# Half-size weight sums moved to VectorE, squares to ScalarE, and seven products for four more chunks of the MLP

## The chip, the cores and the metric

One core of a Trainium2 chip runs the whole program. The metric is the device time of one launch in microseconds, as the median of several runs.

## The reference

Two layers work on x, 512 rows of 1024 numbers in float32. Each layer computes three kinds of attention from x, merges them by gates, projects the result and normalises. Then comes the MLP, which is what this change touches:

```
ff = square(relu(x @ w_up[layer])) @ w_down[layer]
x = layer_norm(alpha * x + ff, ln2_g[layer], ln2_b[layer])
```

`w_up` is 1024 x 4096 and `w_down` is 4096 x 1024.

## The kernel before, in words

**Numbers.** TensorE multiplies in a rounded float32 format. To keep float32 precision, each operand is held as a rounded part and a remainder (`Split`, line 42), and each product is three matmuls, hi by hi, hi by lo and lo by hi (`mm3`, lines 152 to 155). A full matmul has 128 x 128 stationary numbers and 512 moving columns.

**The stream of weights.** All weights come through one list (`Stream`, line 164). A weight of 128 x 1024 is loaded into a `raw` tile (two exist), split by ScalarE into `whi` (line 182) and by VectorE into `wlo` (line 183), and taken by the matmuls. There are five pairs of `whi` and `wlo` in one pool and three in another, so splits may run up to eight weights ahead. `take` (line 213) hands out one weight, and through `advance` (line 201) it writes down the next split and the next load. An entry of the list may also be a function, which then makes its own tile; `Fast` uses that.

**The MLP of a layer.** The 4096 hidden features go in four quarters of eight chunks of 128 (loop at line 898). For each chunk m, 24 matmuls make `psu` (line 933), and `hidden` (line 901) turns it into stationary operands: ScalarE applies Relu (line 910), VectorE squares in place (line 911), and the result lies in `f`, of which one buffer exists for a pair of chunks. In the first quarter the first four chunks are done in two halves of tokens (`cut`, line 925), so that their results come close together.

**The down projection.** In quarters 0 to 2 it uses seven products of halves in place of eight (`Fast`, line 765): the matrix of hidden values and the weights are each cut in two by two blocks, and seven products of sums of blocks are enough. The sums of the hidden blocks are made on VectorE in `hidden` (lines 918 to 922). The sums of weight blocks are made by GpSimd, one subtraction of two 128 x 1024 tiles at a time, in place (`operand`, line 784, subtraction in line 796):

```
dst, a, b = ((b11, None, None), (b11, b12, b11), (b11, b22, b11), (b22, None, None),
             (b12, b22, b12), (b12, None, None), (b11, b12, b11))[i]
if a is not None:
    nc.gpsimd.tensor_tensor(dst, a, b, op=ALU.subtract)
```

A quarter loads eight `w_fast` tiles and uses 14 weights (seven products, two tiles each). `run` (line 802) makes each product with two times four times three matmuls and adds it from PSUM to x (`add_stats`, line 259, on VectorE), two sums per product. The first product needs, as its fourth stationary operand, the slice that `hidden` makes of chunk 6.

In the last quarter all eight chunks go the plain way (`token_major`, line 737): 8 chunks, 4 token blocks, 2 halves, 3 matmuls each. The first four weights are used one after the other, the last four are held, so that the token blocks end one by one and their normalisation starts early.

**What sets the order.** Per engine the program order, with the list of weights as written in lines 855 to 859; loads are issued from the queue of SyncE (SP). The tile framework places independent instructions of one engine earlier or later when it builds the program.

**Places in memory.** Small tiles are rounded up to 64 bytes (`LINE`, line 39), so every tile starts at a multiple of 64 bytes.

Of the kernel before, what the change touches and what calls it, by code (L numbers as in the profile page):

```python
# [17 lines left out]
P = 128  # L18
L = 2
# [17 lines left out]
C_OFF = {0: 0, 1: 256, 2: 640, 3: 1024}  # L37
C_WID = 1280
LINE = 16


class Split:
# [84 lines left out]

@with_exitstack
def encoder(ctx: ExitStack, tc: tile.TileContext, x, x_t, w_qkv, w_c, w_gate, b_gate, qn, kn, rpb,
            w_ba, w_bb, w_bc, w_out, ln1_g, ln1_b, w_up, w_down, w_fast, ln2_g, ln2_b,  # L130
            mask_a, rope_a, rope_b, out):
    nc = tc.nc
    const = ctx.enter_context(tc.tile_pool(name="const", bufs=1))
# [1 line left out]
    glob = ctx.enter_context(tc.tile_pool(name="glob", bufs=1))  # L135
    dram = ctx.enter_context(tc.tile_pool(name="dram", bufs=1, space=bass.MemoryType.DRAM))
    edge = ctx.enter_context(tc.tile_pool(name="edge", bufs=1, side="right"))
    edge.tile([P, LINE // 2], F32, name="edge")
    psum = ctx.enter_context(tc.tile_pool(name="psum", bufs=8, space=bass.MemoryType.PSUM))

    def bank(name):
# [2 lines left out]
    def f32(ap):  # L144
        return ap.bitcast(F32)

    ident = const.tile([P, P], F32, name="ident")
    make_identity(nc, ident)
    nhalf = const.tile([P, 16], F32, name="nhalf")
    nc.vector.memset(nhalf, -0.5)  # L150

    def mm3(ps, lhs, rhs, start, stop, again=False):
# [145 lines left out]
    def attention(l, keep, qk, open_heads):  # L298
# [72 lines left out]
        def norm_rotate(tb):  # L371

            raw = raws["b"][:, tb]
            r = raw.rearrange("p (h d) -> p h d", d=HD)
            sq = pool.tile([P, 10, HD], F32, tag="sq", name="sq", bufs=2)
            nc.scalar.activation(sq, r, AF.Square)
            cs = pool.tile([P, 2, 2, HD], F32, tag="cs", name="cs", bufs=1)
            nc.vector.tensor_tensor(cs, gqk, ropeb[:, :, tb][:, None].to_broadcast([P, 2, 2, HD]), op=ALU.mult)
            yield 1
            ss = pool.tile([P, 2, LINE], F32, tag="ss", name="ss", bufs=2)[:, :, :10]  # L380
            nc.vector.tensor_reduce(ss[:, 0], sq, axis=AX.X, op=ALU.add)
            nc.vector.tensor_scalar(ss[:, 0], ss[:, 0], 1.0 / HD, RMS_EPS, op0=ALU.mult, op1=ALU.add)
# [127 lines left out]
        def scores(name, h, qb):  # L510
            ks, qs = pairs[name, h // 2]
            q, k = qs[h % 2], ks[h % 2]
            k0, k1 = keys_of(name, qb)
            n = (k1 - k0) * P
            ps = bank("pss")[:, :n]
            nc.tensor.matmul(ps, q[:, qb * P:(qb + 1) * P], k.hi[:, k0 * P:k1 * P], start=True, stop=False)
            nc.tensor.matmul(ps, q[:, qb * P:(qb + 1) * P], k.lo[:, k0 * P:k1 * P], start=False, stop=True)
            p = pool.tile([P, S], F32, tag="p", name="p", bufs=4)[:, :n]
            st = pool.tile([P, LINE], F32, tag="stat", name="stat", bufs=4)
            if name == "b":  # L520
                s = ps
# [12 lines left out]
            return p, normalize  # L534
# [115 lines left out]
        with tc.manual_schedule() if l == 0 else nullcontext():  # L650
            work.flush()
        pool = open_heads()
        hb = keep.tile([P, 4 * KB], F32, tag="hb", name="hb")[:, :3 * KB]
        nc.sync.dma_start(hb, b_gate[l])
        nc.vector.tensor_scalar(hb, hb, 0.5, None, op0=ALU.mult)
        gqk = pool.tile([P, 2, 2, HD], F32, tag="gqk", name="gqk", bufs=1)
# [108 lines left out]
    class Fast:  # L765
# [6 lines left out]
        ORDER = ((1, 0, "x", (0, 0)), (4, 1, "z", (1, 1)), (5, 2, "x", (0, 1)), (7, 3, "z", (0, 1)),  # L772
                 (6, 4, "x", (1, 1)), (3, 5, "y", (0, 0)), (2, 6, "x", (1, 0)))

        def __init__(self, pools, src):
            self.pools, self.src = pools, src
            self.b = {}

        def load(self, quarter, half, into):
            t = self.pools["mlp"].tile([P, 1024], F32, tag=f"b{into}{half}", name="braw")  # L780
            nc.sync.dma_start(t, self.src[quarter, half])
            self.b[into, half] = t

        def operand(self, i, half):

            if i == 0 and half == 0:
                for quarter in (0, 1, 3):
                    for h in range(2):
                        self.load(quarter, h, quarter)
            if i == 5:  # L790
                self.load(2, half, 1)
            b11, b12, b22 = (self.b[k, half] for k in (0, 1, 3))
            dst, a, b = ((b11, None, None), (b11, b12, b11), (b11, b22, b11), (b22, None, None),
                         (b12, b22, b12), (b12, None, None), (b11, b12, b11))[i]
            if a is not None:
                nc.gpsimd.tensor_tensor(dst, a, b, op=ALU.subtract)  # L796
            return dst

        def items(self):
            return [lambda i=i, half=half: self.operand(i, half) for i in range(7) for half in range(2)]  # L800

        def run(self, hid, done):
            ps = {}
            for a, _, name, (i, n) in self.ORDER:
                w = [stream.take(2) for _ in range(2)]
                new = name not in ps
                if new:
                    ps[name] = [bank("psd") for _ in range(2)]
                for t in range(2):
                    for j in range(4):  # L810
                        lhs = hid[j].map(lambda h: h[:, a - 1, t * P:(t + 1) * P])
                        mm3(ps[name][t], lhs, w[j // 2][:, j % 2], new and j == 0, j == 3, True)
# [24 lines left out]
    for l in range(L):  # L837
        with ExitStack() as left:
# [12 lines left out]
            extra[0] = pool(right, "wts", "right")  # L851
            stream.plan([w_out[l, k] for k in range(KB)], [0] * 4 + [1] * 3 + [0])
            pools = {}
            fast = [Fast(pools, w_fast[l, q]) for q in range(3)]
            plan = []
            for q in range(4):
                plan += [w_up[l, q * 8 + m] for m in range(8)]
                plan += fast[q].items() if q < 3 else [w_down[l, m] for m in range(8)]
            stream.plan(plan, [int(m % 8 in (1, 4, 6)) for m in range(len(plan) - 4)] + [1] * 3 + [0])
            if l < L - 1:  # L860
                stream.plan([w_qkv[l + 1, i] for i in range(6)])
# [36 lines left out]
            for q in range(4):  # L898
                hid, sums = [], []

                def hidden(m, ps):
# [6 lines left out]
                    a = 2 * (m % 2)  # L908
                    r = f[:, a:a + 2]
                    nc.scalar.activation(r, ps.rearrange("p (a n) -> p a n", a=2), AF.Relu)  # L910
                    nc.vector.tensor_tensor(r, r, r, op=ALU.mult)
                    if q == 3:
                        split_psum(h.map(lambda t: t[:, a:a + 2]), r)
                    elif a == 0:
                        split_psum(h.map(lambda t: t[:, 0]), f[:, 1])
# [8 lines left out]
                for m0 in range(0, 8, 4):  # L924
                    cut = [(0, 2), (2, 4)] if q == 0 and m0 == 0 else [(0, 4)]
                    ws, ps = [], []
                    for a, b in cut:
                        for i in range(4):
# [8 lines left out]
                            elif i in (0, 2):  # L937
                                late.popleft()()

                if q < 3:  # L940
                    def add(tb, n, ps):
                        add_stats(mlp, xs[tb], ps, n, 1.0 if (tb, n) in started else ALPHA, None)
                        started.add((tb, n))

                    fast[q].run(sums, add)
                    continue

                st = [stats_tile(mlp) for _ in range(TB)]
# [13 lines left out]
                        late.popleft()()  # L962

                stream.burst = 2
                whole = [h.map(lambda t: t[:, 2 * i:2 * i + 2].rearrange("p a n -> p (a n)")) for h in sums for i in range(2)]
                token_major(whole, 8, half_done, done, between)
                stream.burst = 1
    right.close()

# [52 lines left out]
    return w.reshape(k // P // per, per, P, n).transpose(0, 2, 1, 3).reshape(-1, P, 1024)  # L1022


def _quarters(w):

    w = w[:, :24 * P].reshape(L, 3, 2, 2, 2, P, 2, 512).transpose(0, 1, 4, 6, 2, 5, 3, 7)
    return w.reshape(L, 3, 4, 2, P, 1024)


def _swap(g):
# [50 lines left out]
```

## Time and profile before

| | |
|---|---|
| median of 3 runs | 1533.81 us (1532.96 to 1535.28) |
| the profiled execution | 1538.57 us, of which 1536.8 us from the first to the last instruction |
| TensorE (PE) busy | 1501.1 us, 98% |
| VectorE (DVE) busy | 1096.1 us, 71% |
| ScalarE (ACT) busy | 688.0 us, 45% |
| GpSimd (POOL) busy | 311.6 us, 20% |

PE is the matmul engine, PEld its loads of stationary operands. The names `psd<-whi,hh` mean: written tile, then the tiles read. `psu` is the up projection, `psd` an output or down projection, `psg` a gate, `hh` and `hl` the two parts of a hidden operand, `braw` a `w_fast` tile, `raw` any other weight. L183 is line 183. TensorE's own durations overlap, so its pace is read from the starts of the matmuls.

### The profile page before, as it was taken

The page shows a single profiled execution, that of the slowest core. Times are in us where ns is not written, and L with a number is a line of the kernel's source. Part 1 is how long each engine was busy: PE and PEld are TensorE (multiplying, and loading weights), DVE is VectorE, ACT ScalarE, POOL GpSimd, SP SyncE. Part 2 cuts the span into 40 slices and gives each one's busy share as a digit, 9 for nine tenths or more (in the row PEclk, how much of TensorE's full clock was granted, in tenths as well). Part 3 has the DMA queues.
Part 4 walks back from the last instruction along what each step waited for, and adds up shares of the span by engine and source line. Part 5 has one row for each costly group of instructions (what it writes and reads, how often), then busy time and mean ns, then how long its engine had stood idle before and what let it go on. Part 6 is the DMA issues. An engine that isn't in the chain of part 4 may idle for free.

```text
span 1536.8 us, 19258 instructions
## 1 busy us (share of the span) xinstructions
PE 1501.1 (98%) x7256; PEld 1255.7 (82%) x7256; DVE 1096.1 (71%) x1722; ACT 688.0 (45%) x1096; POOL 311.6 (20%) x238
## 2 busy tenths in 40 slices
PE   7999999999998999999999999999999989999997
PEld 6888888888896888888888888888888968888886
DVE  4677977745588797964666787876447888979636
ACT  4565656533134343433236556565332343535320
POOL 0112212311142222210101141233111413222001
PEclk9999999999998999999999999999999999999999
DMA  6222321143242415042331323112441342340411
GB/s 218 84 79 70 112 68 53 58 164 118 75 178 81 139 56 164 1 131 85 114 129 56 99 77 110 55 55 76 160 133 56 152 137 83 91 129 28 138 55 55
DMA packets 43438, 150.63 MB, mean 98 GB/s; under 512 B 5073, under 2 KB 5713, under 8 KB 43345
## 3 DMA queue, kind: packets, MB, share of 16 engines
q1 hardware_dynamic: 43344, 149.40, 30.8%
q8 instruction: 57, 0.93, 0.2%
q14 instruction: 37, 0.30, 0.1%
HBM read 145.19 MB, written 4.19 MB: 97 GB/s over the span
## 4 chain that ended last, share of the span: by engine, by line
PE 88%; DVE 7%; ACT 2%; issue 1%; DMA 1%; POOL 0%; SPq 0%; POOLq 0%; DVEq 0%; ACTq 0%
PE psd L153 8%; PE psd L154 8%; PE psd L155 8%; PE psu L154 6%; PE psu L153 6%; PE psu L155 6%; PE psg L155 6%; PE psg L154 6%; PE psg L153 6%; PE psp L547 3%; PE psq L153 2%; PE psq L155 2%; PE psq L154 2%; DVE wlo L183 2%; PE psb L155 2%; PE psb L153 2%
## 5 line engine op out<-in xcount | busy, mean ns | idle before, releaser
L183 DVE TENSOR_TENSOR wlo<-raw,whi 128x1024 fp32r<-128x1024 f32 (+1 forms) x198 | 247.9, 1253 | 204.2 <-ACT whi L182 201.9
L182 ACT ACTIVATE whi<-raw 128x1024 fp32r<-128x1024 f32 (+1 forms) x198 | 207.7, 1051 | 268.7 <-DMA raw<-in_w_up 110.6
L153 PE MATMUL psu<-xTh,whi 128*128 128x512 f32 (+1 forms) x576 | 210.8, 366 | 0.0
L154 PE MATMUL psu<-xTl,whi 128*128 128x512 f32 (+1 forms) x576 | 210.7, 366 | 0.0
L155 PE MATMUL psu<-xTh,wlo 128*128 128x512 f32 (+1 forms) x576 | 210.4, 365 | 0.0
L153 PE MATMUL psd<-whi,hh 128*128 128x512 f32 x464 | 183.2, 395 | 14.8 <-ACT hh L231 14.8
L796 POOL TENSOR_TENSOR braw<-braw 128x1024 f32<-128x1024 f32 x48 | 130.1, 2713 | 332.7 <-DVE wlo L183 169.2
L154 PE MATMUL psd<-wlo,hh 128*128 128x512 f32 x464 | 182.3, 393 | 0.0
L155 PE MATMUL psd<-whi,hl 128*128 128x512 f32 x464 | 182.2, 393 | 0.0
L153 PE MATMUL psg<-xTh,whi 128*128 128x512 f32 x384 | 156.7, 408 | 0.0
L155 PE MATMUL psg<-xTh,wlo 128*128 128x512 f32 x384 | 151.6, 395 | 0.0
L154 PE MATMUL psg<-xTl,whi 128*128 128x512 f32 x384 | 151.5, 395 | 0.0
L532 POOL TENSOR_SCALAR p<-p,stat 128x512 f32<-128x512 f32 x96 | 70.4, 734 | 361.5 <-DVE stat L531 247.1
L183 DVE TENSOR_TENSOR wlo<-braw,whi 128x1024 fp32r<-128x1024 f32 x84 | 126.7, 1508 | 18.3 <-ACT whi L182 16.7
L231 ACT ACTIVATE hh<-f 128x768 fp32r<-128x768 f32 (+2 forms) x88 | 60.8, 691 | 144.8 <-DVE f L918 79.4
L153 PEld LDWEIGHTS psu<-xTh,whi 128*128 128x128 f32 x576 | 108.6, 189 | 17.5
L154 PEld LDWEIGHTS psu<-xTl,whi 128*128 128x128 f32 x576 | 108.6, 189 | 17.5
L155 PEld LDWEIGHTS psu<-xTh,wlo 128*128 128x128 f32 x576 | 108.6, 189 | 17.5
L153 PEld LDWEIGHTS psd<-whi,hh 128*128 128x128 f32 x464 | 88.3, 190 | 34.8 <-ACT hh L231 16.5
L182 ACT ACTIVATE whi<-braw 128x1024 fp32r<-128x1024 f32 x84 | 87.9, 1051 | 47.9 <-DMA braw<-in_w_fast 25.3
L155 PEld LDWEIGHTS psd<-whi,hl 128*128 128x128 f32 x464 | 88.1, 190 | 18.9 <-DVE hl L232 0.5
L154 PEld LDWEIGHTS psd<-wlo,hh 128*128 128x128 f32 x464 | 88.3, 190 | 18.3
(121 smaller groups left out, 2991.3 us busy)
## 6 DMA issues: line engine op xcount, KB each, us to landing
raw<-in_w_up SPq DMA_DIRECT2D x64, 512.0 KB, 3.7
raw<-in_w_gate SPq DMA_DIRECT2D x48, 512.0 KB, 3.6
braw<-in_w_fast SPq DMA_DIRECT2D x48, 512.0 KB, 3.7
raw<-in_w_qkv SPq DMA_DIRECT2D x22, 512.0 KB, 3.6
raw<-in_w_out SPq DMA_DIRECT2D x16, 512.0 KB, 3.5
raw<-in_w_down SPq DMA_DIRECT2D x16, 512.0 KB, 3.5
raw<-in_w_c SPq DMA_DIRECT2D x12, 512.0 KB, 3.6
bias<-in_rpb SPq DMA_DIRECT2D x8, 640.0 KB, 4.0
```

Of the source, the lines that this page charges most:

```text
L153: nc.tensor.matmul(ps, lhs.hi, rhs.hi, start=start, stop=False, skip_group_check=again)
L154: nc.tensor.matmul(ps, lhs.hi, rhs.lo, start=False, stop=False, skip_group_check=again)
L155: nc.tensor.matmul(ps, lhs.lo, rhs.hi, start=False, stop=stop, skip_group_check=again)
L182: nc.scalar.activation(hi[:, s], raw[:, s], AF.Copy)
L183: nc.vector.tensor_tensor(lo[:, s], raw[:, s], f32(hi[:, s]), op=ALU.subtract)
L231: nc.scalar.activation(dst.hi, ps, AF.Copy)
L532: (nc.vector if name == "c" else nc.gpsimd).tensor_scalar(p, p, st[:, 3:4], 1.0, op0=ALU.mult, op1=ALU.mult)
L547: nc.tensor.transpose(ps[:, j * P:(j + 1) * P], p[:, j * P:(j + 1) * P], ident)
L796: nc.gpsimd.tensor_tensor(dst, a, b, op=ALU.subtract)
```

## The change

The subtraction of weight tiles goes from GpSimd to VectorE. The squares go from VectorE's product to ScalarE's Square. Four of the last eight chunks of each layer go by `Fast` too, with one tile per block (`tiles` is 1) in place of two. These four chunks get their own array, `w_last`. The padding of small tiles goes from 64 to 512 bytes, and two fillers move the starts of all tiles to multiples of 512 bytes. The diff, cut to its core:

```
+ROW = 128
...
-    edge.tile([P, LINE // 2], F32, name="edge")
+    edge.tile([P, ROW - LINE // 2], F32, name="edge")
...
+    const.tile([P, 3 * ROW // 4], F32, name="pad")
     ident = const.tile([P, P], F32, name="ident")
...
-            ss = pool.tile([P, 2, LINE], F32, tag="ss", name="ss", bufs=2)[:, :, :10]
+            ss = pool.tile([P, 2, ROW // 2], F32, tag="ss", name="ss", bufs=2)[:, :, :10]
...
-            st = pool.tile([P, LINE], F32, tag="stat", name="stat", bufs=4)
+            st = pool.tile([P, ROW], F32, tag="stat", name="stat", bufs=4)
...
-        def __init__(self, pools, src):
-            self.pools, self.src = pools, src
+        def __init__(self, pools, src, tiles):
+            self.pools, self.src, self.tiles = pools, src, tiles
...
         def operand(self, i, half):
+            one = self.tiles == 1
             if i == 0 and half == 0:
...
+                for name, quarter in (("x", 0), ("y", 1), ("w", 3)):
+                    for h in range(self.tiles):
+                        self.load(quarter, f"{name}{h}")
+                if one:
+                    self.b["y1"], self.b["x1"] = self.room("y1"), self.room("x1")
+                    nc.sync.dma_start(self.b["y1"], self.src[2, 0])
+            if i == 5 and not one:
+                self.load(2, f"y{half}")
+            x, y, w = (self.b[f"{name}{half}"] for name in "xyw")
+
+            t1, last, b21 = (self.b["x1"], self.b["x1"], self.b["y1"]) if one else (x, x, y)
+            dst, a, b = ((x, None, None), (t1, y, x), (x, w, t1), (w, None, None),
+                         (y, w, y), (b21, None, None), (last, b21, x))[i]
             if a is not None:
-                nc.gpsimd.tensor_tensor(dst, a, b, op=ALU.subtract)
+                nc.vector.tensor_tensor(dst, a, b, op=ALU.subtract)
             return dst
...
-                w = [stream.take(2) for _ in range(2)]
+                w = [stream.take(2) for _ in range(self.tiles)]
...
-                    for j in range(4):
+                    for j in range(2 * self.tiles):
...
-            fast = [Fast(pools, w_fast[l, q]) for q in range(3)]
+            fast = [Fast(pools, w_fast[l, q], 2) for q in range(3)] + [Fast(pools, w_last[l], 1)]
             plan = []
             for q in range(4):
                 plan += [w_up[l, q * 8 + m] for m in range(8)]
-                plan += fast[q].items() if q < 3 else [w_down[l, m] for m in range(8)]
+                plan += fast[q].items()
+            plan += [w_down[l, m] for m in range(4)]
...
-                    nc.vector.tensor_tensor(r, r, r, op=ALU.mult)
-                    if q == 3:
+                    nc.scalar.activation(r, r, AF.Square)
+                    if q == 3 and m > 3:
...
+                fast[q].run(sums, add)
                 if q < 3:
...
-                whole = [h.map(lambda t: t[:, 2 * i:2 * i + 2].rearrange("p a n -> p (a n)")) for h in sums for i in range(2)]
-                token_major(whole, 8, half_done, done, between)
+                whole = [h.map(lambda t: t[:, 2 * i:2 * i + 2].rearrange("p a n -> p (a n)")) for h in sums[2:] for i in range(2)]
+                token_major(whole, 4, half_done, done, between)
```

## Rows read from the trace of the kernel before

**Rows 1.** The page: the engines, then the chain that ended last by engine

```profile
PE 1501.1 (98%) x7256; PEld 1255.7 (82%) x7256; DVE 1096.1 (71%) x1722; ACT 688.0 (45%) x1096; POOL 311.6 (20%) x238
...
PE 88%; DVE 7%; ACT 2%; issue 1%; DMA 1%; POOL 0%; SPq 0%; POOLq 0%; DVEq 0%; ACTq 0%
```

**Rows 2.** The waits, TensorE alone: us in total, times, longest us

```profile
PE psd L153 <- ACT hh L231: 14.8, 3, 7.4
```

**Rows 3.** The timeline of TensorE, layer 0, first quarter: start us, us, what, [idle before]

```profile
470.34 0.39 PE L153 MATMUL psd<-whi,hh 128*128 128x512 f32 x1
...
472.15 0.39 PE L155 MATMUL psd<-whi,hl 128*128 128x512 f32 x1
479.61 0.80 PE L153 MATMUL psd<-whi,hh 128*128 128x512 f32 x1 [7.07 <-ACT hh L231]
...
485.59 0.40 PE L155 MATMUL psd<-whi,hl 128*128 128x512 f32 x1
```

**Rows 4.** The same timeline, layer 1, first quarter

```profile
1231.52 0.39 PE L155 MATMUL psd<-whi,hl 128*128 128x512 f32 x1
1239.27 0.80 PE L153 MATMUL psd<-whi,hh 128*128 128x512 f32 x1 [7.36 <-ACT hh L231]
...
1243.45 0.40 PE L154 MATMUL psd<-wlo,hh 128*128 128x512 f32 x1
```

**Rows 5.** The timeline of VectorE in layer 0's first quarter

```profile
447.36 2.51 DVE L918 TENSOR_TENSOR f<-f 128x256 f32<-128x256 f32 x1
...
453.92 4.02 DVE L232 TENSOR_TENSOR hl<-f,hh 128x768 fp32r<-128x768 f32 x2
...
478.42 0.68 DVE L911 TENSOR_TENSOR f<-f 128x512 f32<-128x512 f32 x1
```

**Rows 6.** The stretches: window, us, busy of PE PEld DVE ACT POOL, PEclk, DMA, GB/s

```profile
440.00:470.30 30.30, 30.30 (x169) 26.58 (x168) 28.64 (x25) 11.74 (x16) 16.74 (x6) 1.00 0.23 93
479.61:485.32 5.71, 5.71 (x13) 4.47 (x14) 5.15 (x9) 3.54 (x5) 0.00 (x0) 0.50 0.58 182
518.51:561.00 42.49, 42.49 (x189) 35.21 (x188) 38.61 (x37) 18.33 (x24) 15.99 (x6) 1.00 0.13 39
561.00:599.00 38.00, 38.00 (x170) 31.46 (x169) 30.44 (x35) 15.86 (x19) 5.73 (x2) 1.00 0.54 167
```

**Rows 7.** The groups of instructions by form: busy us, mean ns, then idle before

```profile
L183 DVE TENSOR_TENSOR wlo<-braw,whi 128x1024 fp32r<-128x1024 f32 x84 | 126.7, 1508 | 18.3 <-ACT whi L182 16.7 <-DMA raw<-in_w_up 0.5 <-PE psu L154 0.5
L796 POOL TENSOR_TENSOR braw<-braw 128x1024 f32<-128x1024 f32 x48 | 130.1, 2713 | 332.7 <-DVE wlo L183 169.2 <-DMA braw<-in_w_fast 162.8
L921 DVE TENSOR_TENSOR f<-f 128x256 f32<-128x256 f32 x72 | 59.5, 828 | 1.9
L918 DVE TENSOR_TENSOR f<-f 128x256 f32<-128x256 f32 x24 | 31.0, 1290 | 0.8
```

**Rows 8.** One tile's instructions, f then braw: duration ns min/median/max

```profile
L918 DVE TENSOR_TENSOR f<-f x24: 410/426/2512, 447.4 to 1408.0; 128x256 f32<-128x256 f32 x24
...
L183 DVE TENSOR_TENSOR wlo<-braw,whi x84: 1209/1224/3415, 441.8 to 1424.6; 128x1024 fp32r<-128x1024 f32 x84
...
DMA to landing us min/median/max: 3.4/3.7/9.9
```

**Rows 9.** The groups by form again: the sums into x, the copies of f

```profile
L259 DVE SCALAR_TENSOR_TENSOR x<-x,psd 128x512 f32<-128x512 f32 x116 | 77.9, 679 | 12.1 <-PE psd L155 12.0
...
L231 ACT ACTIVATE hh<-f 128x512 fp32r<-128x512 f32 x16 | 10.1, 633 | 19.9 <-DVE f L911 19.9
```

**Rows 10.** The groups by form again: a matmul of the up stage, one of the gates

```profile
L155 PE MATMUL psu<-xTh,wlo 128*128 128x512 f32 x448 | 174.3, 389 | 0.0
...
L155 PE MATMUL psg<-xTh,wlo 128*128 128x512 f32 x384 | 151.6, 395 | 0.0
```

**Rows 11.** The waits for w_fast loads, POOL then ACT: us in total, times, longest

```profile
POOL braw L796 <- DMA braw<-in_w_fast: 162.8, 11, 25.8
...
ACT whi L182 <- DMA braw<-in_w_fast: 25.3, 11, 3.0
```

More of the change, by code (lines that the diff above doesn't have):

```diff
@@ L129, in encoder @@
 def encoder(ctx: ExitStack, tc: tile.TileContext, x, x_t, w_qkv, w_c, w_gate, b_gate, qn, kn, rpb,
-            w_ba, w_bb, w_bc, w_out, ln1_g, ln1_b, w_up, w_down, w_fast, ln2_g, ln2_b,
+            w_ba, w_bb, w_bc, w_out, ln1_g, ln1_b, w_up, w_down, w_fast, w_last, ln2_g, ln2_b,
             mask_a, rope_a, rope_b, out):
@@ L145, in f32 @@
         return ap.bitcast(F32)
+    const.tile([P, 3 * ROW // 4], F32, name="pad")
     ident = const.tile([P, P], F32, name="ident")
     make_identity(nc, ident)
-    nhalf = const.tile([P, 16], F32, name="nhalf")
+    nhalf = const.tile([P, ROW], F32, name="nhalf")[:, :16]
     nc.vector.memset(nhalf, -0.5)
@@ L652, in attention @@
         pool = open_heads()
-        hb = keep.tile([P, 4 * KB], F32, tag="hb", name="hb")[:, :3 * KB]
+        hb = keep.tile([P, ROW], F32, tag="hb", name="hb")[:, :3 * KB]
         nc.sync.dma_start(hb, b_gate[l])
@@ L773, in encoder, with room @@
                  (6, 4, "x", (1, 1)), (3, 5, "y", (0, 0)), (2, 6, "x", (1, 0)))
-        def __init__(self, pools, src):
-            self.pools, self.src = pools, src
+        def __init__(self, pools, src, tiles):
+            self.pools, self.src, self.tiles = pools, src, tiles
             self.b = {}
[L779 to L782, printed above, removed]
+        def room(self, name):
+            return self.pools["mlp"].tile([P, 1024], F32, tag=f"b{name}", name="braw")
@@ L784, in operand, with load @@
+        def load(self, quarter, name):
+            self.b[name] = t = self.room(name)
+            nc.sync.dma_start(t, self.src[quarter, int(name[1])])
         def operand(self, i, half):
+            one = self.tiles == 1
             if i == 0 and half == 0:
[L787 to L792, printed above, removed]
@@ L793, in operand @@
-            dst, a, b = ((b11, None, None), (b11, b12, b11), (b11, b22, b11), (b22, None, None),
-                         (b12, b22, b12), (b12, None, None), (b11, b12, b11))[i]
+                for name, quarter in (("x", 0), ("y", 1), ("w", 3)):
[4 more added lines that the diff above has]
+                    nc.sync.dma_start(self.b["y1"], self.src[2, 0])
@@ L797, in operand @@
             return dst
         def items(self):
-            return [lambda i=i, half=half: self.operand(i, half) for i in range(7) for half in range(2)]
+            return [lambda i=i, half=half: self.operand(i, half) for i in range(7) for half in range(self.tiles)]
         def run(self, hid, done):
@@ L809, in run @@
                 for t in range(2):
-                    for j in range(4):
+                    for j in range(2 * self.tiles):
                         lhs = hid[j].map(lambda h: h[:, a - 1, t * P:(t + 1) * P])
-                        mm3(ps[name][t], lhs, w[j // 2][:, j % 2], new and j == 0, j == 3, True)
+                        mm3(ps[name][t], lhs, w[j // 2][:, j % 2], new and j == 0, j == 2 * self.tiles - 1, True)
                     done(2 * (1 - i) + t, n, ps[name][t])
@@ L938, in encoder, with add @@
                                 late.popleft()()
+                def add(tb, n, ps):
+                    add_stats(mlp, xs[tb], ps, n, 1.0 if (tb, n) in started else ALPHA, None)
+                    started.add((tb, n))
+                fast[q].run(sums, add)
                 if q < 3:
[L941 to L945, printed above, removed]
                     continue
@@ L1022, in _by_rows, with _quarters @@
     return w.reshape(k // P // per, per, P, n).transpose(0, 2, 1, 3).reshape(-1, P, 1024)
-def _quarters(w):
-    w = w[:, :24 * P].reshape(L, 3, 2, 2, 2, P, 2, 512).transpose(0, 1, 4, 6, 2, 5, 3, 7)
-    return w.reshape(L, 3, 4, 2, P, 1024)
+def _quarters(w, groups, tiles):
+    w = w.reshape(L, groups, tiles, 2, 2, P, 2, 512).transpose(0, 1, 4, 6, 2, 5, 3, 7)
+    return w.reshape(L, groups, 4, tiles, P, 1024)
 def _swap(g):
@@ L1068 @@
         "w_up": np.stack([_by_features(w, P) for w in given["w_up"]]),
-        "w_down": given["w_down"].reshape(L, FF // P, P, D)[:, 24:],
-        "w_fast": _quarters(given["w_down"]),
+        "w_down": given["w_down"].reshape(L, FF // P, P, D)[:, 28:],
+        "w_fast": _quarters(given["w_down"][:, :24 * P], 3, 2),
+        "w_last": _quarters(given["w_down"][:, 24 * P:28 * P], 1, 1)[:, 0],
         "ln2_g": given["ln2_g"], "ln2_b": given["ln2_b"],
```

## The prediction

> **What bounds the kernel now.** I read the page first. TensorE is busy 98% of the span, and 88% of the chain that ended last lies on it [rows 1]. So the time is matmuls times their pace, plus the places where TensorE stands still. Busy time is not pace, so I took the pace from the timeline: from 470.34 to 472.15 us lie eight steps, 0.226 us each [rows 3].
>
> Next I asked who keeps TensorE waiting. In the MLP it waits for one thing only, a hidden slice `hh`: three waits, 14.8 us [rows 2]. The timeline shows the two long ones, 7.07 us in layer 0 and 7.36 us in layer 1, both at the first product of the first quarter [rows 3, 4]. The third is the rest, 0.4 us. Each long one also costs clock. After the first the granted clock is 0.50, the lower level of 1.2 GHz, for 5.71 us [rows 6]. I price the whole from starts: 472.15 to 485.59 us holds 15 steps, at 0.226 worth 3.4 us, so 10.0 us are lost; 1231.52 to 1243.45 holds 11 steps, worth 2.5 us, so 9.4 us are lost [rows 3, 4].
>
> Then I asked why `hh` is late. VectorE is busy 28.64 of 30.30 us in the stretch before the first wait, and GpSimd runs six weight subtractions there, 16.74 us [rows 6]. VectorE's own rows show what these do. A 128x256 operation takes 2.51 us where the median is 0.426 us, and a pair of 0.95 us copies takes 4.02 us [rows 5, 8]. So each GpSimd subtraction holds up one VectorE operation by about 2.1 us. The square of chunk 6, on which TensorE waits, runs at 478.42 us [rows 5], six us after TensorE wanted its slice.
>
> **The change part by part.**
>
> *Seven products for four more chunks.* The last quarter had 8 chunks x 4 x 2 x 3 = 192 matmuls. It gets 7 x 2 x 2 x 3 = 84 by products and 4 x 4 x 2 x 3 = 96 plain: 12 fewer per layer, 24 in all. 24 x 0.226 = **5.4 us** on the path. What it adds is VectorE work beside TensorE: 14 more sums into x per layer, 28 x 0.68 = 19 us [rows 9], and 16 small hidden sums x 0.43 = 7 us. The bytes loaded stay the same (four `w_last` tiles for four `w_down`). The last token blocks run as before, 12 matmuls each with four held weights, so the end of the program keeps its length.
>
> *Subtractions on VectorE.* 48 plus 8 new ones. VectorE has no such row; its nearest is `wlo`, same shape, two inputs in memory, median 1.224 us [rows 8]. 56 x 1.224 = 69 us more. In exchange the hold-ups go: 126.7 - 84 x 1.224 = 24, 31.0 - 24 x 0.426 = 21, 59.5 - 72 x 0.426 = 29, together 74 us [rows 7, 8]. The move is even for VectorE, and GpSimd loses its 130 us [rows 7]. The Trainium skill, SBUF — State Buffer, section "Who interferes with whom", says that a VectorE instruction with two inputs in SBUF contends with a GpSimd instruction that reads SBUF, and that the second to issue waits for the whole of the first. By that rule VectorE could get back all of GpSimd's 130 us; the rows show 74, and neither figure is in the sum.
>
> *Squares on ScalarE.* VectorE sheds 64 x 0.68 = 44 us [rows 5]. ScalarE has no such square; the nearest row, a copy of 128x512 within `f`, takes 0.633 us [rows 9], so it gains 41 us on 688 [rows 1]. The chain Relu, square is as long as before and loses a hand-over; I cost it at nothing. If the cover were gone, each chunk would be 0.05 us better.
>
> *What this does to the wait.* In the 30.30 us stretch VectorE sheds six hold-ups (12.5 us) and about six squares (4.1 us), and takes six subtractions (7.3 us): 28.6 becomes 19.3 us. `hh` came 7.1 us too late, and 9.3 us are freed in front of it. So I expect both long waits gone, with the low clock behind them, and the third too: 10.0 + 9.4 + 0.4 = **19.8 us**. The margin is only 2 us; that is the second rival. `f` has one buffer, so a pair's chain must end before the next Relu; it is shorter by the same hold-ups.
>
> *Whether VectorE then becomes the bound.* An up stretch has 38.61 us of VectorE in 42.49; without six hold-ups and eight squares and with six subtractions it has 28. A stretch of products has 30.44 in 38.00 [rows 6]; with two of each exchanged, 29. Only the new short products are tight. One takes TensorE 12 x 0.226 = 2.7 us, and VectorE a split, two sums and 4/7 of a subtraction, 1.22 + 1.36 + 0.70 = 3.3 us. Seven fall 4 us behind per layer, 8 us in all, if nothing is done ahead. But splits do run ahead: the first `braw` split starts at 441.8 us [rows 8], 28 us before its product. Bounds 0 and 8; I take 1, near the first, because the quarter before them is the emptiest on VectorE.
>
> *Queues.* The subtraction now stands in VectorE's program order, and what waits behind it are sums into x, hidden work and splits. SP's queue issues as many loads as before; in the new quarter its fourth `w_last` load comes at once with the first three, into a tile of its own. ScalarE's splits wait for subtractions as before, now 1.2 instead of 2.7 us long.
>
> *Multiples of 512 bytes.* No row has such a tile. The same `xT` and `whi` tiles give 389 ns in the up stage and 395 ns among the gates [rows 10], so address is not what parts them; I take 0. The bound for gain is 6 ns on 3 x 384 gate matmuls, 7 us; nothing excludes as much loss, 7 us. The Trainium skill, SBUF — State Buffer, section "Specifications (TRN2)", puts full bandwidth on 16-byte lines, which tiles at 64 bytes already meet: by it, 0. [...]
>
> **Sum.** 5.4 + 19.8 - 1 = 24.2 us. The profiled execution took 1538.57 us, so 1514.4 us on its terms. It lies 4.8 us above the median of the runs, 1533.81; I take the same 24.2 us from the median: **1509.6 us**. VectorE should show about 1096 + 69 - 74 - 44 + 19 + 7 = 1073 us.
>
> **The rivals.**
>
> *The long waits shrink by half.* VectorE is freed in total, but the four hidden chunks of the first group still come close together, and six subtractions now stand in the same queue as their chain. If 3.5 us are left per layer, the low clock comes along, some 2.5 us: 12 us of the 19.8 stay, 1521.6 us. For it: the margin of 2 us. Against: the freed time lies before the slice. Chance 0.16.
>
> *The short products give back what they save.* The full 8 us of lag shows: 1516.6 us. For it: 3.3 against 2.7 us. Against: the splits made ahead. Chance 0.09.
>
> *The start of tiles matters* to the gates: 7 us more gained, 1502.6 us. Chance 0.06.
>
> *VectorE waits for loads: slower than before.* GpSimd waited 162.8 us in 11 waits for the `w_fast` loads [rows 11], and that cost nothing. On VectorE the first subtraction of each of 8 quarters would hold every sum and split behind it. TensorE has a cover of one product, 24 x 0.226 = 5.4 us; the slowest load took 9.9 us [rows 8], leaving 4.5 us, plus 2.5 of clock: 8 x 7 = 56 us, 1566 us. It decides from 3 us lost per quarter. Against: the split of the first tile stands ahead of the subtraction, and ScalarE waits at most 3.0 us for the same loads [rows 11]. Chance 0.08.
>
> **How the numbers follow.** The forecast as argued has 0.56, and 0.05 is left for what none of these names. About 0.2% (3 us) is what a measurement can tell from no change. Faster by more: the forecast and the first three rivals, 0.56 + 0.16 + 0.09 + 0.06 = 0.87. Slower: the last rival's 0.08 and 0.01 of the unnamed; within: the other 0.04. The range from 1502 to 1521.5 us takes in the forecast with its bounds and nearly all of the second and third cases.
>
> **What would show it.** TensorE without a wait for `hh` above 1 us and a granted clock of 1.00 after 470 us; 24 `psd` matmuls fewer; the 128x256 operations on VectorE near 0.43 us on average; no GpSimd subtraction; VectorE near 1073 us. A wait of TensorE for `wlo`, or a long wait of VectorE for `in_w_fast`, would prove the forecast wrong.

## The result and the profile after

The changed kernel took 1508.53 us (median of 4 runs, 1505.88 to 1508.86), the kernel before beside it 1534.55 us (4 runs, 1532.96 to 1537.35). The ratio is 0.9825, with a 95% interval of 0.9806 to 0.9843: 26.0 us faster by the medians. The forecast was 1509.6 us, with a range of 1502 to 1521.5. The profiled execution after took 1508.48 us, its span 1506.6 us; the one before had taken 1538.57 us, some 4 us above its median.

First the page of the kernel after, its engines and the chain that ended last; it answers to [rows 1].

```profile
PE 1485.4 (99%) x7232; PEld 1247.2 (83%) x7232; DVE 1060.8 (70%) x1768; ACT 738.1 (49%) x1170; POOL 181.4 (12%) x190
...
PE 96%; DVE 2%; DMA 1%; ACT 1%; issue 0%; POOL 0%; SPq 0%; POOLq 0%; DVEq 0%; ACTq 0%
```

TensorE has 24 matmuls fewer, and now 96% of the chain lies on it, where it was 88%. VectorE is busy 35 us less: it gave up the squares, but took on all the subtractions. What TensorE still waits for, with the total, the number of waits and the longest, answers to [rows 2]:

```profile
PE psq L155 <- ACT whi L184: 6.5, 1, 6.5
PE psp L549 <- POOL p L534: 4.7, 2, 2.4
PE psq L155 <- ACT xTh L835: 1.3, 1, 1.3
PE psq L157 <- DVE xTl L836: 0.5, 1, 0.5
```

The 14.8 us for `hh` are gone; the first line is the start of the program. The windows show where they went: the 30.34 us before the first product of the first quarter of layer 0, this quarter's products, and the last quarter's down projection of layer 1. They answer to [rows 6].

```profile
core 0: us, PE busy (x) PEld busy (x) DVE busy (x) ACT busy (x) POOL busy (x), PEclk, DMA share, GB/s
437.70:468.04 30.34, 30.34 (x169) 26.58 (x168) 26.23 (x36) 20.80 (x32) 0.00 (x0) 1.00 0.29 111
468.04:506.12 38.08, 38.08 (x169) 31.53 (x168) 28.60 (x33) 16.37 (x17) 0.00 (x0) 1.00 0.56 171
1457.60:1498.40 40.80, 40.80 (x181) 33.60 (x179) 31.68 (x48) 5.86 (x7) 4.50 (x3) 1.00 0.15 52
```

The quarter's 168 matmuls take 38.08 us, 0.227 each, and the clock stays at 1.00, the level of 2.4 GHz; before, the same 168 took 48.17 us. The stages, worked out from the starts of TensorE's matmuls on the timeline of both profiles:

| stage | before, us | after, us | gained |
|---|---|---|---|
| products, first quarter, layers 0 and 1 | 48.17 and 47.56 | 38.08 and 38.08 | 19.6 |
| products, second and third quarters, both layers | 38.08, 38.13, 38.36, 38.78 | 38.08 each | 1.0 |
| last quarter's down projection | 45.30 and 43.29 | 42.63 and 40.57 | 5.4 |
| attention up to the output projection | 371.41 and 367.16 | 369.60 and 365.37 | 3.6 |
| up stages, first quarter, layers 0 and 1 | 46.63 each | 46.64 and 46.65 | 0 |
| up stages, other quarters (six) | 43.52 each | 43.52 each | 0 |

These make 29.6 of the 30.2 us by which the two spans differ. The line of attention is the least sure, since single executions scatter there. Over six profiles with the old starts of tiles (this one and five experiments below) its two stages sum to 735.6 to 738.6 us, 736.9 on average; over six with the new starts, to 732.4 to 735.0 us, 734.0 on average. So 2.8 us of the 3.6 are borne out, and the rest lies in this one execution of before.

How near was it? Here is VectorE's timeline of the kernel after, with the first of six subtractions of the stretch and the slice of chunk 6; a row has start, duration, engine, line, operation. It answers to [rows 5].

```profile
441.20 1.22 DVE L806 TENSOR_TENSOR braw<-braw 128x1024 f32<-128x1024 f32 x1
...
466.34 0.42 DVE L234 TENSOR_TENSOR hl<-f,hh 128x256 fp32r<-128x256 f32 x1
```

And TensorE's timeline after, with the first matmul of the product and the one that waited before; it answers to [rows 3].

```profile
468.04 0.39 PE L155 MATMUL psd<-whi,hh 128*128 128x512 f32 x1
...
470.08 0.39 PE L155 MATMUL psd<-whi,hh 128*128 128x512 f32 x1
```

The first product starts at 468.04 us and reaches this operand at 470.08; the slice is complete at 466.76 (466.34 + 0.42). Before, the product stood still at that place until 479.61 [rows 3]. Now it has 3.3 us in hand.

Last, the groups by line. Each has the number of instructions, the total and the mean in ns, then the idle time before them and what ended it. They answer to [rows 7 to 9].

```profile
L806 DVE TENSOR_TENSOR braw<-braw 128x1024 f32<-128x1024 f32 x56 | 67.9, 1219 | 7.3 <-DMA braw<-in_w_last 3.8 <-DMA braw<-in_w_fast 3.5
L185 DVE TENSOR_TENSOR wlo<-braw,whi 128x1024 fp32r<-128x1024 f32 x98 | 119.6, 1223 | 73.5 <-ACT whi L184 73.2
L932 DVE TENSOR_TENSOR f<-f 128x256 f32<-128x256 f32 x84 | 35.1, 422 | 3.3 <-ACT f L922 2.4
L929 DVE TENSOR_TENSOR f<-f 128x256 f32<-128x256 f32 x28 | 11.9, 424 | 0.0
L922 ACT ACTIVATE f<-f 128x512 f32<-128x512 f32 x64 | 40.3, 633 | 1.8
```

The 128x256 operations had meant 828 and 1290 ns and now mean 422 and 424; the `braw` splits went from 1508 to 1223. The subtraction costs VectorE 1219 ns where GpSimd took 2713. The idle time of the first row matters too: VectorE waited 7.3 us for loads in 56 subtractions, and TensorE waited for none of it.

### The profile page after: what moved, and what is told of

Same layout as the page of the kernel before. It is cut to its first block, busy times and chain, and to the rows that moved or that the text cites. A ratio compares the mean times of both kernels' runs of the same rounds, so it can differ in the third digit from the quotient of the medians.

```text
span 1506.6 us, 19237 instructions
## 1 busy us (share of the span) xinstructions
PE 1485.4 (99%) x7232; PEld 1247.2 (83%) x7232; DVE 1060.8 (70%) x1768; ACT 738.1 (49%) x1170; POOL 181.4 (12%) x190
## 4 chain that ended last, share of the span: by engine, by line
PE 96%; DVE 2%; DMA 1%; ACT 1%; issue 0%; POOL 0%; SPq 0%; POOLq 0%; DVEq 0%; ACTq 0%
PE psd L156 8%; PE psd L157 8%; PE psd L155 8%; PE psu L156 8%; PE psu L157 8%; PE psu L155 8%; PE psg L157 6%; PE psg L156 6%; PE psg L155 6%; PE psp L549 3%; PE psq L157 3%; PE psq L155 3%; PE psq L156 3%; PE psb L155 2%; PE psb L157 2%; PE psb L156 2%
## 5 line engine op out<-in xcount | busy, mean ns | idle before, releaser
L185 DVE TENSOR_TENSOR wlo<-raw,whi 128x1024 fp32r<-128x1024 f32 (+1 forms) x190 | 237.9, 1253 | 158.5 <-ACT whi L184 153.9
L184 ACT ACTIVATE whi<-raw 128x1024 fp32r<-128x1024 f32 (+1 forms) x190 | 199.0, 1050 | 254.0 <-DMA raw<-in_w_up 109.8
L155 PE MATMUL psd<-whi,hh 128*128 128x512 f32 x456 | 177.6, 389 | 0.0
L157 PE MATMUL psd<-whi,hl 128*128 128x512 f32 x456 | 177.4, 389 | 0.0
L156 PE MATMUL psd<-wlo,hh 128*128 128x512 f32 x456 | 177.4, 389 | 0.0
L185 DVE TENSOR_TENSOR wlo<-braw,whi 128x1024 fp32r<-128x1024 f32 x98 | 119.6, 1223 | 73.5 <-ACT whi L184 73.2
L184 ACT ACTIVATE whi<-braw 128x1024 fp32r<-128x1024 f32 x98 | 103.8, 1059 | 116.6 <-PE psu L156 72.7
L271 POOL TENSOR_TENSOR ve<-ve,nhalf 128x1 f32<-128x1 f32 x16 | 24.1, 1507 | 739.1 <-DVE ve L270 739.1
L261 DVE SCALAR_TENSOR_TENSOR x<-x,psd 128x512 f32<-128x512 f32 x144 | 97.2, 681 | 17.8 <-PE psd L157 17.2
```

The source lines that it names most:

```text
L155: nc.tensor.matmul(ps, lhs.hi, rhs.hi, start=start, stop=False, skip_group_check=again)
L156: nc.tensor.matmul(ps, lhs.hi, rhs.lo, start=False, stop=False, skip_group_check=again)
L157: nc.tensor.matmul(ps, lhs.lo, rhs.hi, start=False, stop=stop, skip_group_check=again)
L184: nc.scalar.activation(hi[:, s], raw[:, s], AF.Copy)
L185: nc.vector.tensor_tensor(lo[:, s], raw[:, s], f32(hi[:, s]), op=ALU.subtract)
L261: nc.vector.scalar_tensor_tensor(z[:, s], z[:, s], scale, ps, op0=ALU.mult, op1=ALU.add)
```

## The experiments

The theory: the time comes from GpSimd's subtractions, which read memory and so hold up VectorE's operations with two inputs; with them goes the wait for `hh`. The rivals: the squares did it; the places of the tiles did it; the seven products did more or less than 24 matmuls.

### Each part alone

The subtractions alone, in the kernel before:

```
-                nc.gpsimd.tensor_tensor(dst, a, b, op=ALU.subtract)
+                nc.vector.tensor_tensor(dst, a, b, op=ALU.subtract)
```

> The kernel before with one part of the change alone: the weight subtractions on VectorE. My theory: GpSimd's hold-ups were most of what made the hidden slice late, 12.5 of the 16.6 us of VectorE time in front of it that the whole change sheds, against 7.3 us of subtractions taken on. So 5.2 us are freed where 7.1 were missing: the two long waits of TensorE shrink to at most 2 us each, most of their low clock goes, and the time falls by 14 to 20 us (ratio 0.987 to 0.991). Rival: VectorE only changes one load for another, and both long waits stay above 5 us; the time falls by under 8 us.

Measured: 1515.23 us, ratio 0.9876 [0.9861 to 0.9891], 19.3 us by the medians. TensorE no longer waits for `hh` by over 0.1 us; the two first quarters' products take 38.18 and 38.17 us, 0.1 above the pace. So this edit alone takes away both long waits, only just: on its timeline the slice of chunk 6 is complete at 471.57 us, and the product that starts at 468.94 reaches it about then.

The squares alone:

```
-                    nc.vector.tensor_tensor(r, r, r, op=ALU.mult)
+                    nc.scalar.activation(r, r, AF.Square)
```

> The kernel before with the squares on ScalarE and nothing else. My theory: about six squares, 4.1 us, leave VectorE ahead of the late slice and the hold-ups stay, so the two long waits fall from 7.1 and 7.4 us to about 3 us each, with the low clock mostly kept: 6 to 10 us faster (ratio 0.9935 to 0.996). Rival: a hold-up takes whatever operation stands next, so the chain of hold-ups sets the slice and nothing is gained: within 2 us.

Measured: 1525.41 us, 0.9938 [0.9926 to 0.9951], 9.1 us. One line of its waits of TensorE:

```profile
PE psd L153 <- ACT hh L231: 6.3, 2, 3.2
```

Half of the wait is left, in two waits of about 3 us as expected, and the products take 42.85 and 43.15 us. This too acts on the wait for `hh`, so its gain and that of the subtractions can't be added.

The tiles alone (`ROW` of 128 numbers for the padded tiles, and the two fillers `edge` and `pad`):

```
-    edge.tile([P, LINE // 2], F32, name="edge")
+    edge.tile([P, ROW - LINE // 2], F32, name="edge")
+    const.tile([P, 3 * ROW // 4], F32, name="pad")
-    nhalf = const.tile([P, 16], F32, name="nhalf")
+    nhalf = const.tile([P, ROW], F32, name="nhalf")[:, :16]
...
```

> The kernel before with every tile at a multiple of 512 bytes and nothing else. The changed kernel's attention stages were 1.8 us shorter in each layer, which the prediction had put at 0. If the starts of tiles did that, these stages are 1.8 us shorter here too and the time falls by 3 to 4 us (ratio 0.9975). If the chip varies by that much from run to run, or another part did it, the time is within 1 us.

Measured: 1531.06 us (11 runs), 0.9979 [0.9970 to 0.9988], 3.5 us. The waits for `hh` stand as before, 14.4 us in three. The branch projections run quicker, here by line, with the mean ns behind the total:

```profile
L155 PE MATMUL psb<-oh,whi 128*128 128x512 f32 x128 | 51.7, 404 | 0.0
L157 PE MATMUL psb<-oh,wlo 128*128 128x512 f32 x128 | 50.1, 391 | 0.0
L156 PE MATMUL psb<-ol,whi 128*128 128x512 f32 x128 | 50.0, 391 | 0.0
```

In the kernel before the same three read 407, 395 and 393 ns. Durations overlap, so here is the pace as well, as the mean step from one start to the next at full clock: a branch matmul went from 232.7 to 228.4 ns, a gate matmul from 229.8 to 228.7. For 384 and 1152 of them that is 1.6 and 1.2 us. The steps of the branch are the same within 0.1 ns in every profile with the old starts of tiles, and in every profile with the new. The two stages of attention of this run take 368.81 and 363.59 us.

The seven products for four more chunks alone (`Fast` with one tile per block, `w_last`):

```
+            fast = [Fast(pools, w_fast[l, q], 2) for q in range(3)] + [Fast(pools, w_last[l], 1)]
...
+            plan += [w_down[l, m] for m in range(4)]
```

> The kernel before with four of each layer's last eight chunks by seven products, subtractions left on GpSimd, squares on VectorE, tiles at 64 bytes. My theory: 24 matmuls at 0.226 us, 5.4 us faster (ratio 0.9965), the long waits of the first quarter unchanged. Rival: with GpSimd's slow subtractions, 2.7 us each against a product of 2.7 us, the short products wait for weights and give the 5.4 us back or more: within 1 us, or slower.

Measured: 1530.66 us, 0.9977 [0.9966 to 0.9988], 3.9 us by the medians, 1.8 to 5.2 by the interval. The last quarters' down projections get shorter by 2.52 and 2.72 us, together 5.24, and the waits for `hh` are 14.9 us in four. So in their own stages the products give what 24 matmuls cost even with the subtractions on GpSimd. The whole time gives 1 to 2 us less; the interval all but reaches 5.24, so this may be noise.

Subtractions, tiles and products add up to 19.3 + 3.5 + 3.9 = 26.7 us, and the whole change gave 26.0. With the squares' 9.1 the sum would be 35.8.

### One part taken back

The squares taken back to VectorE, all else as changed:

> The changed kernel with the squares back on VectorE. My theory after the single parts: the subtractions alone end the long waits (0.1 us is left of each), so the squares have nothing left to remove: within 1.5 us of the changed kernel, ratio to the kernel before 0.982 to 0.984. Rival: the short products, where VectorE had 3.3 us of work for 2.7 us of TensorE, need the room that the squares give, and TensorE waits there: 3 to 8 us slower than the changed kernel, 0.985 to 0.988.

Measured: 1505.88 us, 0.9802 [0.9789 to 0.9816]; no wait for `hh`, first products 38.18 and 38.17 us. To compare it, the changed kernel was run once more:

> The changed kernel itself, once more, beside the kernel before: what the comparison gives for the same program on another occasion. 0.981 to 0.984, and by it the difference to the kernel with squares on VectorE (0.9802) is judged: if it comes out at 0.980 to 0.982, the place of the squares is worth nothing; at 0.9835 or above, they cost on ScalarE.

Measured: 1507.02 us, 0.9815 [0.9802 to 0.9829]. The two intervals overlap: with the subtractions on VectorE, the place of the squares is worth nothing that can be measured.

The tiles taken back:

> The changed kernel with tiles at 64 bytes again. If the starts of tiles are worth what they were worth alone (0.9979), this is 2 to 4.5 us slower than the changed kernel, ratio 0.984 to 0.9855, all of it in the attention stages. If that gain was another part's, it is within 1 us of 0.9825.

Measured: 1510.57 us, 0.9838 [0.9824 to 0.9851]; the branch matmuls are back at 407, 395 and 393 ns. It lies 2 to 3.5 us above the changed kernel, in the direction of the tiles' own 3.5, but the intervals touch, so by its time alone this run proves nothing. Its trace says more: the branch step is back at 232.7 ns, and the 3.4 us between its span (1510.0 us) and that of the changed kernel all lie in the two stages of attention, 738.5 us against 735.0.

The subtractions taken back to GpSimd, all else as changed:

> The changed kernel with the weight subtractions back on GpSimd, squares on ScalarE. My theory: the hold-ups are back, 56 of them, and the waits of the first quarters at about 3 us each as with the squares alone; the four chunks and the tiles keep their 5 and 3 us: 8 to 12 us slower than the changed kernel, ratio 0.988 to 0.991. Rival: in the short products GpSimd's 2.7 us per sum also makes TensorE wait for weights: several us more, above 0.992.

Measured: 1515.54 us, 0.9871 [0.9855 to 0.9887], 8.5 us slower than the changed kernel in the same set of runs. Of its waits of TensorE, the one for `hh`:

```profile
PE psd L155 <- ACT hh L233: 6.3, 2, 3.2
```

The wait is that of the squares alone. The last quarters take 42.84 and 40.58 us against 42.63 and 40.57 in the changed kernel, so even with subtractions of 2.7 us the short products keep up.

### Is it GpSimd's reading, or its work?

In the kernel before, each subtraction on GpSimd was replaced by two fills of the same tile, which write but read nothing. The sums of weights are left out, so the products use constant weights in their place:

```
-                nc.gpsimd.tensor_tensor(dst, a, b, op=ALU.subtract)
+                nc.gpsimd.memset(dst, 0.01)
+                nc.gpsimd.memset(dst, 0.02)
```

> The kernel before, where GpSimd makes each weight sum by two fills of the tile in place of one subtraction (the sums are left out, so the output is another one): about as long on GpSimd, but it reads nothing. My theory: no hold-up of VectorE, 128x256 operations at 0.43 us, both long waits under 1 us, as with the subtractions on VectorE: ratio 0.986 to 0.989. Rival: the length of GpSimd's step in the chain of the weights makes the waits: they stay above 5 us, ratio above 0.995.

Measured: 1514.63 us, 0.9864 [0.9850 to 0.9877]. GpSimd keeps its place in the order, waits for the same tiles, and is busy 1.9 us per sum instead of 2.7. The groups by line:

```profile
L796 POOL MEMSET braw<- 128x1024 f32 x48 | 45.7, 957 | 300.3 <-DVE wlo L183 206.6 <-DMA braw<-in_w_fast 93.1 <-issue 0.6
...
L922 DVE TENSOR_TENSOR f<-f 128x256 f32<-128x256 f32 x72 | 30.4, 424 | 1.9
L919 DVE TENSOR_TENSOR f<-f 128x256 f32<-128x256 f32 x24 | 10.2, 424 | 0.8
```

VectorE runs free: 424 ns where it was 828 and 1290 [rows 7], and no wait for `hh`. Its busy time falls by 1096.1 - 1008.8 = 87.3 us with none of its work removed, so one subtraction on GpSimd had cost it 87.3 / 48 = 1.8 us on average. The rule of the Trainium skill that the prediction named (SBUF — State Buffer, section "Who interferes with whom") also says that a VectorE instruction with two inputs in SBUF does not contend with a GpSimd instruction that only writes. This trace agrees: 68 of the 96 operations of 128x256 on `f` ran beside a fill, and they too took 424 ns. So the shorter sum (1.9 instead of 2.7 us) is not what brought the 424 ns.

The trace of the kernel before shows the hold-up one operation at a time. The 24 operations of 128x256 on `f` that ran beside a subtraction took 2505 ns on average; the 72 others took 422, none over 430. The sums into x are the control. They read one tile in SBUF, the memory that holds the tiles, and one in PSUM, where matmuls write, and none of the 116 was held, not even the six that ran beside a subtraction (duration ns min/median/max):

```profile
L259 DVE SCALAR_TENSOR_TENSOR x<-x,psd x116: 668/680/689, 403.1 to 1528.8; 128x512 f32<-128x512 f32 x116
```

The other way round, a subtraction on GpSimd was added beside each of VectorE's in the changed kernel. Nothing waits for its result; it overwrites the gain of the last normalisation, so the output is another:

```
                 nc.vector.tensor_tensor(dst, a, b, op=ALU.subtract)
+                nc.gpsimd.tensor_tensor(self.pools["gb"][:, 0], dst, self.pools["gb"][:, 1], op=ALU.subtract)
...
-            pools["mlp"] = mlp
+            pools["mlp"], pools["gb"] = mlp, gb
```

> The changed kernel, and beside each subtraction of VectorE a GpSimd subtraction of the same size that reads the new tile and whose result no product uses (it overwrites the gain of the second normalisation, so the output is another one). My theory: GpSimd's reading alone holds VectorE up. Hold-ups of 2 us or more return on 128x256 operations, and as the squares are on ScalarE the waits of TensorE in the first quarters return at 1 to 4 us: 3 to 12 us slower than the changed kernel. Rival: what made the slice late was that the weight sums themselves took 2.7 us on GpSimd; that is gone here, so no wait returns and the time is within 1 us of the changed kernel.

Measured: 1548.99 us, 1.0083 [1.0064 to 1.0101], about 40 us above the changed kernel and slower than the kernel before. Its waits of TensorE, those for `hh` and for a sum into x:

```profile
PE psd L155 <- ACT hh L233: 28.8, 6, 8.8
...
PE psd L155 <- DVE x L261: 2.2, 2, 1.9
```

And its groups by line, the added subtraction and VectorE's small operations:

```profile
L807 POOL TENSOR_TENSOR gb<-braw,gb 128x1024 f32<-128x1024 f32 x56 | 154.8, 2765 | 418.3 <-DVE braw L806 388.0 <-DMA braw<-in_w_fast 29.1
...
L933 DVE TENSOR_TENSOR f<-f 128x256 f32<-128x256 f32 x84 | 78.2, 934 | 4.3 <-ACT f L923 3.4
L930 DVE TENSOR_TENSOR f<-f 128x256 f32<-128x256 f32 x28 | 25.0, 891 | 0.0
```

VectorE's busy time rises by 1168.1 - 1060.8 = 107 us, 1.9 us for each of the 56, and the wait for `hh` is back, in six places where the kernel before had three. The products of the six quarters with two tiles per block take 49.69, 42.41, 42.42, 49.43, 42.27 and 44.87 us, together 42.6 above the pace, which is the whole loss. The sums into x stay at 680 ns. The mechanism is shown from both sides. The size was expected at 3 to 12 us: what VectorE can bear before `hh` is late was over-rated, since it now carries the subtractions and the hold-ups together.

### What it is about the tiles

The padding alone, without the two fillers, in the kernel before. Three small tiles of the normalisation, `mv`, `ve` and `st`, keep their 64 bytes in the code of this and all the other kernels. By the sizes, the tiles of the left side then start 128 bytes past a multiple of 512, where they had started 192 past (the expectation says 192, which overlooked that `nhalf` grows too):

```
+ROW = 128
-    nhalf = const.tile([P, 16], F32, name="nhalf")
+    nhalf = const.tile([P, ROW], F32, name="nhalf")[:, :16]
...
```

> The kernel before with the small tiles rounded up to 512 bytes, but without the two fillers: tiles then start 192 bytes past a multiple of 512 in place of at it. If the start at a multiple of 512 is what made the tiles part 0.9979, this one is within 1 us of the kernel before, and the branch matmuls keep their 395, 393 and 407 ns. If it is that small tiles no longer share 512 bytes, the gain of about 3 us is here too.

Measured: 1540.35 us, 1.0034 [1.0022 to 1.0047], 5 us slower. The branch matmuls are as quick as with the fillers, 404, 391 and 391 ns, and the stages of attention as short, 732.4 us together. But now others are slower. The window of one up stage, from its first matmul to the first of the products, with the columns of the windows above:

```profile
513.88:557.98 44.10, 44.10 (x194) 36.05 (x193) 40.23 (x40) 19.07 (x25) 16.01 (x6) 1.00 0.13 40
```

And its group by line of the matmuls in the up stages:

```profile
L155 PE MATMUL psu<-xTl,whi 128*128 128x512 f32 x448 | 175.6, 392 | 0.0
```

The six up stages of the second to last quarters take 44.08 to 44.10 us at full clock, against 43.52 in all the other kernels, and the mean is 392 ns against 389: together they lose 3.4 us. They are not alone. The output projections take 46.24 us instead of 45.33, the last quarters 45.91 and 43.95 instead of 45.30 and 43.29, and the products of the second and third quarters 38.72 and 38.78, where the pace gives 38.08. With the up stages that is about 9 us lost, against some 4.5 gained in attention. The same instructions on the same data run 1.3% slower in an up stage because tiles lie elsewhere. So where tiles start does set TensorE's pace, in both directions. Which relation of the addresses decides (of operands to each other, or to a multiple of 512) was not tried.

### A faster version

With the wait for `hh` gone, the next wait inside the program is `psp` for the divided probabilities on GpSimd, 4.7 us in two. Here the first two blocks of each layer are divided on VectorE, and the squares stay on VectorE as well:

```
-                (nc.vector if name == "c" else nc.gpsimd).tensor_scalar(p, p, ...)
+                (nc.vector if name == "c" or (name, h) == ("a", 0) and qb < 2 else nc.gpsimd).tensor_scalar(p, p, ...)
```

> The changed kernel with the squares back on VectorE, and the division of the first two blocks of probabilities of each layer on VectorE in place of GpSimd. There TensorE still waits 4.4 us in two waits, because GpSimd's division stands behind a two-input split of VectorE. My theory: about 1.2 us of each wait goes, and perhaps part of the low clock behind it: 2 to 5 us less than the kernel with squares on VectorE, ratio 0.977 to 0.979. Rival: the split of a weight, now second on VectorE, is what TensorE then waits for, and nothing is gained.

Measured: 1502.55 us, 0.9786 [0.9773 to 0.9799], against 1507.02 for the changed kernel in the same set of runs. Of its waits of TensorE, that for the probabilities:

```profile
PE psp L549 <- DVE p L534: 1.7, 2, 1.2
```

The wait is 1.7 us instead of 4.4 in the kernel with the squares on VectorE, and the mean granted clock is 0.999 instead of 0.996: two stretches of 3.4 us at a granted clock of 0.50, one behind each of these waits, are gone. In the profiles the two stages of attention fall from 735.0 to 728.6 us. It beats both the kernel before and the changed kernel. How much of it the division gives is less sure by the times, since the interval overlaps that of the kernel with only the squares back on VectorE (0.9789 to 0.9816).

## Why the prediction was right

**What bounds the kernel, and why `hh` is late.** Held. The wait and the low clock behind it are gone, and the run with fills and the run with the added reader show that GpSimd's reading held VectorE up.

**The wait, 19.8 us.** The first quarters gained 10.1 and 9.5 us, the other quarters 1.0: 20.6. The third, short wait had been put at 0.4 and was 0.4; the rest of the 1.0 are slow steps of TensorE right behind it and in another quarter, while the granted clock stayed at 1.00. VectorE's own sum for the 30 us stretch was not what came: 26.2 us instead of 19.3, because it did 36 instructions there where it had done 25; the freed time was filled with other work. The forecast needed only that the slice be early, and it is by 3.3 us against a margin worked out as 2. Its numbers for the parts hold as well: with the squares alone they leave 7.1 - 4.1 = 3.0 us of wait, and 3.2 were measured; with the subtractions alone they leave 7.1 - (12.5 - 7.3) = 1.9 us, and no more than 0.1 was left.

**Squares.** Costed at nothing on the chain and 44 us off VectorE. The first held; the second came out at 41 us alone and 37.5 in the changed kernel (1098.3 - 1060.8). ScalarE's square takes 633 ns, as its copy did. What the text did not say is that the squares and the subtractions pay for the same wait: the squares are worth 9 us alone and nothing after the subtractions.

**Hold-ups, 74 us.** Too small: 87.3. The step added up three groups [rows 7]; left out were the operations that make `hl` and the squares, slowed in the same way. In the groups by line of the kernel before they read:

```profile
L232 DVE TENSOR_TENSOR hl<-f,hh 128x768 fp32r<-128x768 f32 x48 | 49.7, 1047 | 0.2
L911 DVE TENSOR_TENSOR f<-f 128x512 f32<-128x512 f32 x64 | 48.0, 753 | 12.2 <-ACT f L910 12.1
...
L232 DVE TENSOR_TENSOR hl<-f,hh 128x256 fp32r<-128x256 f32 x24 | 18.9, 788 | 0.3
```

Against the 957, 685 and 425 ns that they take beside the fills, this is 4.3 + 4.4 + 8.7 = 17 us by single durations, which overlap a little. These are part of why VectorE shows 1060.8 us and not 1073. On the other side the forecast left out six more splits that the new products need (198 + 84 before, 190 + 98 after), 7 us on VectorE; the two were not separated further. Each subtraction held VectorE up by 1.8 us on average, not 2.1: the text had read that from the worst places. Of GpSimd's 130 us, which the prediction named as the most that could come back, 87 came.

**Seven products, 5.4 us, less 1 for short products.** 2.67 + 2.72 = 5.39 us by the stages. The lag of 1 us is not there, and with GpSimd's slow sums it is no more than 0.2 us. That rival falls.

**Multiples of 512 bytes, 0 us.** This is the step that failed. It measured 3.5 us, 0.9979 [0.9970 to 0.9988]. The argument was that address is not what parts the paces, since the same tiles are read in the up stage at 389 ns and among the gates at 395. But a matmul reads two tiles and writes a third, and moving them changes the pace of some stages and not of others: the step of the branch went from 232.7 to 228.4 ns, that of the gates only from 229.8 to 228.7, that of the up stages not at all. The bounds, 7 us each way, held what came, a gain of 3.5 and, with other places, a loss of 5. The rule of the Trainium skill that the prediction drew on here (SBUF — State Buffer, section "Specifications (TRN2)", 16-byte lines), which gave 0, does not account for either. With this term at 3.5, the waits at 20.6 and no lag, the sum by terms would be 5.4 + 20.6 + 3.5 = 29.5 us. The profiled executions differ by 30.1 (1538.57 to 1508.48), the medians by 26.0, within 24.1 to 29.8 by the interval. That the forecast of 24.2 came so near the medians is in part luck: the terms were 5.3 us too small together, and against that the profiled execution of before, from which the losses were taken as they stood, is 4 us longer than its median.

**The rivals.** The long waits did not shrink by half, they went; by half is what the squares alone give. The start of tiles matters, but the gates, which the rival named, got 1.2 us of its 7, and each branch matmul gained four times as much as a gate matmul. VectorE does wait for loads, 7.3 us in all, never long enough to cross TensorE's cover of one product; so nothing was left of the slower case.

## What to carry to other kernels

When an engine that should be fast enough is late, compare its mean durations with its medians: a group whose mean is twice its median is likely being held up, and the holder is looked for among what runs beside it. A group that reads in another way, like the sums into x here, is the control. Moving the holder's work onto the held engine can make that engine less busy: with the subtractions alone moved, VectorE had 48 instructions more and was busy 1056.0 us instead of 1096.1. Parts of a change that shorten the same wait are worth the larger of them, not the sum.

## What was not expected of the hardware

- Where tiles start changes the pace of matmuls at full clock by 1 to 2%: up stages of 43.52 or 44.10 us, branch matmuls 232.7 or 228.4 ns from start to start. No wait and no idle time shows it; only the pace does.
- A GpSimd instruction that reads two tiles for 2.7 us cost VectorE 1.8 to 1.9 us on average, even where nothing waits for its result; two fills of 0.96 us cost it nothing that can be seen. The operations that were held read two tiles in SBUF; the sums that read one of theirs from PSUM kept their 680 ns beside the same subtractions.
